# Taking the two-input passes of an attention layer off GpSimd: low weight parts by accumulating transfers, rotations and splits on VectorE

## The chip, the cores and the metric

The kernel runs on one core of a Trainium2 chip. A core has TensorE (matrix products; its weight loads are a second row, PEld, in the profile), VectorE (DVE), ScalarE (ACT), GpSimd (POOL) and SyncE (SP, which issues transfers). Each engine takes its own instructions strictly in the order of the program; engines wait for each other by semaphores. The metric is the time of the program on the device in microseconds (us), the median of several runs.

## The reference

Two layers over 512 positions of width 1024, in float32: a recurrent layer with a feed-forward block, then attention with a feed-forward block. What the change touches is the attention:

```python
k = rms_norm(k, k_norm[:, None, :]);  k = apply_partial_rope(k, cos, sin)      # shared_kv
q = (h @ w_q).reshape(B, S, N_GROUPS, Q_HEADS, HEAD_DIM)      # 3 groups, 8 heads of 128
q = rms_norm(q, q_norm[:, None, :])
q = apply_partial_rope(q, cos, sin)           # the first 32 of 128: x1*c - x2*s, x2*c + x1*s
...
for g, (window, dilation) in enumerate(DILATION_GROUPS):      # (128,1), (512,4), (2048,16)
    o, l = dilated_window_attention(q[:, :, g], k[:, :, g], v[:, :, g], window, dilation)
o = sum over g of softmax(l)[g] * o[g]
return o.reshape(B, S, Q_HEADS * HEAD_DIM) @ w_o
```

## The kernel before

Every product is made of three: each operand is split into a high part (a cast to TensorE's float32 format) and a low part (the rest), and high x high, high x low and low x high are summed. Weights come from DRAM in pieces of 128 x 1024 in one fixed order (`pieces`, a `Stream`): SP loads a piece into `wr` (two buffers, L78), ACT casts it to `wh` (L92), and the low part `wl` is made in one of three ways, by the piece's kind: on VectorE (`wr - wh`, L99), on GpSimd (the same line, kind "pool"), or, kind "dma", by ACT writing the negated cast (L95) and an accumulating transfer that GpSimd issues, which adds the weights from DRAM once more (L96). `wh` and `wl` have three buffers each. `get(i)` asks for the loads up to piece i + 2 and the splits up to piece i + 1. Kind "dma" is used before the change by eight pieces of the recurrent layer; the 24 pieces of `w_q` and the 8 of `w_o` are of kind "pool".

The attention goes so. First keys and values of three groups are projected. Then `project_q(0)` projects the queries of the first key/value head, three groups of four pieces (numbers 104 to 115): 24 products a piece, L641 to L643, from 604 to some 706 us. A group's four results are copied (`kn`, L579), ACT makes 16 sums of squares (`junk`, L583), VectorE the factors (L592, then L196 to L201) and the rotations: per result four scalings (L600) and four small two-input steps (L607 to L610). Each rotated result is transposed by TensorE (L716) and copied by ACT to `qt` (L718). The second head's projection, `project_q(1)` (pieces 116 to 127), is then mixed with the scores and values of the first head (L761 to L816: score tiles `pr`, minima `mn`, sums `den`, their transposes L786 and the split parts `ph`, `pl`), and the second head's scores with the two halves of the output projection (pieces 128 to 135, `out_half`). `query_parts` splits four heads' queries at a time into `qh` and `ql`, 24 times; before the change 16 of the low parts are made on GpSimd. For the second head the steps L607 to L610 (argument `E` of `normed`) are on GpSimd as well, 12 rotations.

The order on each engine is not written out by hand: the program is recorded and then put in order by a scheduler that goes by its own costs, with the splits of the weights at high priority. Names in the rows: `ps` a TensorE result bank, `qr4y` a factor, `grow` the gains, `ra` and `rbt` the small steps' tiles, `kh`/`kl` the keys' parts.

Of the kernel before, what the change touches and what calls it, by code (L numbers as in the profile page):

```python
# [127 lines left out]
def trunk(tc, A, out):  # L128
    nc = tc.nc
    V, S, G, PE = nc.vector, nc.scalar, nc.gpsimd, nc.tensor  # L130
# [9 lines left out]
    def add_pieces(aps, kind="", but=0):  # L140

        start = len(pieces)
        pieces.extend((a, "" if but and i % but == 0 else kind) for i, a in enumerate(aps))
        return start
# [6 lines left out]
    def ffn_pieces(wi, wo):  # L151
        a = add_pieces([A[wi][b] for j in range(HB) for b in (j, HB + j)])
        b = add_pieces([A[wo][m][:, c0:c1] for m in range(8) for c0, c1 in ((0, 1024), (1024, 2048), (2048, 2816))])
        return a, b

    p_f1 = ffn_pieces("f1_in", "f1_out")
    p_kv = add_pieces([A["w_kv"][i] for i in range(12)])
    p_q = add_pieces([A["w_q"][i] for i in range(24)], "pool")
    p_o = add_pieces([A["w_o"][i] for i in range(8)], "pool")
    p_f2 = ffn_pieces("f2_in", "f2_out")  # L160

    with tc.tile_pool(name="keep", bufs=1) as kp, tc.tile_pool(name="wts", bufs=3) as wp, \
# [7 lines left out]
        h = [kp.tile([128, T], F32, name=f"h{k}") for k in range(KB)]  # L170
# [88 lines left out]
        with tc.tile_pool(name="lru", bufs=2) as lp, \  # L259
# [149 lines left out]
            for i, m in enumerate(lru_order):  # L409
# [4 lines left out]
                while xs and xs[0][0] + 2 <= i:  # L414
                    st = xs.pop(0)[1]
# [69 lines left out]
def attention(tc, A, ap, ws, env):  # L485
    nc = tc.nc
    V, S, G, PE = nc.vector, nc.scalar, nc.gpsimd, nc.tensor
    h, xh, xl, ident, ssum = env["h"], env["xh"], env["xl"], env["ident"], env["ssum"]
    bank, mm3, split, halve, rsqrt = env["bank"], env["mm3"], env["split"], env["halve"], env["rsqrt"]
    gain, p_kv, p_q, p_o = env["gain"], env["p_kv"], env["p_q"], env["p_o"]  # L490
# [82 lines left out]
    def collect(raw, nh, t, st, copy):  # L573

        if t == 0:
            st["sq"] = ap.tile([128, 4 * nh], F32, name="sqc", tag=f"sqc{nh}").rearrange("q (t i) -> q t i", i=nh)
            st["kn"] = []
        dst = ap.tile([128, 512], F32, name="kn", tag="kn", bufs=N_KN)
        copy(dst[:, :128 * nh], raw[:, :128 * nh])  # L579
        junk = ap.tile([128, 128], F32, name="junk", tag="ra")  # L580
        for i in range(nh):
            c = slice(128 * i, 128 * i + 128)
            S.activation(junk, dst[:, c], AF.Square, accum_out=st["sq"][:, t, i:i + 1])  # L583
        st["kn"].append(dst)

    def normed(st, nh, tab, g_row, E, turn, lag):

        kn = st["kn"]

        def factors():  # L590
            sq = st["sq"]
            V.scalar_tensor_tensor(sq, sq, 1.0 / 128.0, epsv[:, tab:tab + 4].unsqueeze(2).to_broadcast([128, 4, nh]),  # L592
                                   ALU.mult, ALU.add)
            st["r"] = rsqrt(sq.rearrange("q t i -> q (t i)"), ap, f"qr{nh}")

        def rotate(t):
            dst, r = kn[t], st["r"]
            for i in range(nh):
                c = slice(128 * i, 128 * i + 128)
                V.scalar_tensor_tensor(dst[:, c], dst[:, c], r[:, nh * t + i:nh * t + i + 1], grow[:, g_row, :],  # L600
                                       ALU.mult, ALU.mult)
            x = dst.rearrange("q (h d) -> q h d", d=128)[:, :nh]
            a = ap.tile([128, 4, 32], F32, name="ra", tag="ra")[:, :nh]
            b = ap.tile([128, 4, 32], F32, name="rbt", tag="rbt", bufs=1)[:, :nh]
            cct = cc[:, tab + t].unsqueeze(1).unsqueeze(1).to_broadcast([128, nh, 2, 16])
            sst = [ss[:, tab + t, c, :].unsqueeze(1).to_broadcast([128, nh, 16]) for c in range(2)]
            E.tensor_tensor(*(v.rearrange("q h (c f) -> q h c f", c=2) for v in (a, x[:, :, 0:32])), cct, ALU.mult)  # L607
            E.tensor_tensor(b[:, :, 0:16], x[:, :, 16:32], sst[0], ALU.mult)
            E.tensor_tensor(b[:, :, 16:32], x[:, :, 0:16], sst[1], ALU.mult)
            E.tensor_tensor(x[:, :, 0:32], a, b, ALU.add)  # L610

        at(1, factors)
        for t in range(4):
            at(2 + t, lambda t=t: rotate(t))
            at(lag + t, lambda t=t: turn(t, kn[t]))
# [4 lines left out]
    def at(steps, fn):  # L620
        later.append((now[0] + steps, len(later), fn))
        later.sort(key=lambda e: e[:2])
# [6 lines left out]
    def project(p0, xh, xl, done):  # L629

        ps = [None] * 4
        for kk in range(4):
            wh, wl = ws.get(p0 + kk)
            for t in range(4):
                r = slice(128 * t, 128 * t + 128)
                if kk == 0:
                    ps[t] = bank()
                for k2 in range(2):
                    k = 2 * kk + k2
                    c = slice(512 * k2, 512 * k2 + 512)  # L640
                    PE.matmul(ps[t], xh[k][:, r], wh[:, c], start=k == 0, stop=False)  # L641
                    PE.matmul(ps[t], xh[k][:, r], wl[:, c], start=False, stop=False)  # L642
                    PE.matmul(ps[t], xl[k][:, r], wh[:, c], start=False, stop=k == 7)  # L643
                if kk == 3:
                    done(t, ps[t])
                tick()
                yield
# [58 lines left out]
    qt = {}  # L706

    def project_q(kv):
        for g in range(3):
            def done_q(t, ps, g=g, st={}):  # L710
                collect(ps, 4, t, st, V.tensor_copy)
                if t == 3:
                    def turn(j, rows):
                        pt = bank("PT")
                        for i in range(4):
                            PE.transpose(pt[:, 128 * i:128 * i + 128], rows[:, 128 * i:128 * i + 128], ident)  # L716
                        q = ap.tile([128, 4, 4, 32], F32, name="qt", bufs=12)
                        S.copy(q, pt.rearrange("q (h p i) -> q p h i", h=4, p=4))  # L718
                        qt[j, kv, g] = q

                    normed(st, 4, 0, 3 + g, G if kv else V, turn, 8 + kv)

            yield from project(p_q + 12 * kv + 4 * g, xh, xl, done_q)

# [4 lines left out]
    def query_parts(kv, n):  # L729
        qs_[kv, n] = []  # L730
        for g in range(3):
            if kv and n % 2:
                tags = (f"kh{g}0", f"kl{g}0", 1)
            else:
                tags = ("qh", "ql", 3)
            qh, ql = [ap.tile([128, 512], F32R, name=x, tag=x, bufs=tags[2]) for x in tags[:2]]
            halve(qt.pop((n, kv, g)).rearrange("q p h i -> q (p h i)"), qh, ql, V if g == kv else G)
            qs_[kv, n].append((qh, ql))

    def scores(kv, n, p):  # L740
        if p == 0 and (kv, n) not in qs_:
            query_parts(kv, n)
# [30 lines left out]
        if kv and p == 1 and n < 3:  # L773
            query_parts(kv, n + 1)
# [175 lines left out]
```

## Time and profile before

| | us |
|---|---|
| median of 3 runs (1265.87 to 1271.18) | 1268.6 |
| the profiled execution's own time | 1268.64 |
| its span, first to last instruction | 1266.9 |
| TensorE busy | 1218.9 (96%) |
| VectorE busy | 705.9 (56%) |
| ACT busy | 521.2 (41%) |
| GpSimd busy | 192.6 (15%) |

Busy times overlap; the span is set by the engine that is always needed. An average over the span hides stages: the attention lies between some 540 and 910 us. A timeline row is start, duration, engine, line, operation, output<-inputs, shape and count; in brackets stands how long the engine was idle before it and what ended that. `PEclk` is the granted share of TensorE's clock.

### The profile page before, as it was taken

The page shows a single profiled execution, that of the slowest core. Times are in us where ns is not written, and L with a number is a line of the kernel's source. Part 1 is how long each engine was busy: PE and PEld are TensorE (multiplying, and loading weights), DVE is VectorE, ACT ScalarE, POOL GpSimd, SP SyncE. Part 2 cuts the span into 40 slices and gives each one's busy share as a digit, 9 for nine tenths or more (in the row PEclk, how much of TensorE's full clock was granted, in tenths as well). Part 3 has the DMA queues.
Part 4 walks back from the last instruction along what each step waited for, and adds up shares of the span by engine and source line. Part 5 has one row for each costly group of instructions (what it writes and reads, how often), then busy time and mean ns, then how long its engine had stood idle before and what let it go on. Part 6 is the DMA issues. An engine that isn't in the chain of part 4 may idle for free.

```text
span 1266.9 us, 14906 instructions
## 1 busy us (share of the span) xinstructions
PE 1218.9 (96%) x5634; PEld 1010.3 (80%) x5634; DVE 705.9 (56%) x1292; ACT 521.2 (41%) x964; POOL 192.6 (15%) x172
## 2 busy tenths in 40 slices
PE   7899899999999999999998899899999999999998
PEld 6678688888888888887876777888888888888887
DVE  7788855554455333396566665785754455552221
ACT  5798532332322222266534554554432322332210
POOL 0100001111011000011333355422111011110000
PEclk9899999999999999999999999799999999999999
DMA  5454232223332333332422121001323332223431
GB/s 200 123 135 114 78 100 87 96 100 100 100 100 92 95 93 107 105 102 84 132 68 82 52 67 51 17 18 51 99 85 101 100 100 96 89 94 100 122 119 46
DMA packets 36649, 117.19 MB, mean 93 GB/s; under 512 B 4449, under 2 KB 6625, under 8 KB 36577
## 3 DMA queue, kind: packets, MB, share of 16 engines
q1 hardware_dynamic: 34416, 110.17, 27.6%
q0 software_dynamic: 1152, 4.19, 1.8%
q10 hardware_dynamic: 1008, 1.88, 0.5%
q8 instruction: 44, 0.72, 0.2%
q14 instruction: 29, 0.23, 0.1%
HBM read 113.08 MB, written 2.10 MB: 91 GB/s over the span
## 4 chain that ended last, share of the span: by engine, by line
PE 78%; DVE 12%; ACT 7%; issue 1%; DMA 1%; SPq 0%; DVEq 0%; ACTq 0%
PE ps L135 22%; PE ps L134 22%; PE ps L136 22%; DVE kn L600 3%; PE ps L641 3%; PE ps L643 3%; PE ps L642 3%; ACT junk L583 1%; ACT wh L92 1%; PE ps L716 1%; PE ps L786 1%; DVE kn L610 1%; DVE wl L99 1%; DVE pr L771 1%; DVE gated L386 1%
## 5 line engine op out<-in xcount | busy, mean ns | idle before, releaser
L92 ACT CAST wh<-wr 128x1024 fp32r<-128x1024 f32 (+2 forms) x206 | 210.9, 1024 | 506.8 <-PE ps L135 443.2
L134 PE MATMUL ps<-xh,wh 128*128 128x512 f32 x896 | 353.5, 395 | 12.1 <-ACT xh L205 6.0
L136 PE MATMUL ps<-xh,wl 128*128 128x512 f32 x896 | 351.1, 392 | 0.0
L135 PE MATMUL ps<-xl,wh 128*128 128x512 f32 x896 | 350.8, 391 | 0.0
L99 DVE TENSOR_TENSOR wl<-wr,wh 128x1024 fp32r<-128x1024 f32 (+2 forms) x166 | 240.0, 1447 | 151.9 <-ACT wh L92 151.8
L134 PEld LDWEIGHTS ps<-xh,wh 128*128 128x128 f32 x896 | 169.4, 189 | 48.2 <-DVE xp L332 6.3
L136 PEld LDWEIGHTS ps<-xh,wl 128*128 128x128 f32 x896 | 169.3, 189 | 35.6 <-issue 0.2
L135 PEld LDWEIGHTS ps<-xl,wh 128*128 128x128 f32 x896 | 169.5, 189 | 35.3 <-issue 0.5
L136 PE MATMUL ps<-gh,wl 128*128 128x512 f32 x352 | 137.1, 389 | 0.0
L134 PE MATMUL ps<-gh,wh 128*128 128x512 f32 x352 | 137.1, 389 | 0.0
L135 PE MATMUL ps<-gl,wh 128*128 128x512 f32 x352 | 137.1, 389 | 0.0
L451 POOL TENSOR_TENSOR u<-u,g 128x512 f32<-128x512 f32 x44 | 58.7, 1334 | 507.3 <-ACT wh L92 363.8
L450 DVE TENSOR_TENSOR u<-ps,rb 128x512 f32<-128x512 f32 x44 | 30.4, 691 | 139.2 <-PE ps L136 139.2
L99 POOL TENSOR_TENSOR wl<-wr,wh 128x1024 fp32r<-128x1024 f32 x32 | 77.1, 2409 | 193.2 <-ACT wh L92 141.8
L641 PE MATMUL ps<-wh,xh 128*128 128x512 f32 x224 | 93.2, 416 | 0.0
L643 PE MATMUL ps<-wh,xl 128*128 128x512 f32 x224 | 89.4, 399 | 0.0
L642 PE MATMUL ps<-wl,xh 128*128 128x512 f32 x224 | 89.1, 398 | 0.0
L134 PEld LDWEIGHTS ps<-gh,wh 128*128 128x128 f32 x352 | 66.1, 188 | 13.8
L136 PEld LDWEIGHTS ps<-gh,wl 128*128 128x128 f32 x352 | 66.1, 188 | 13.6
L135 PEld LDWEIGHTS ps<-gl,wh 128*128 128x128 f32 x352 | 66.1, 188 | 13.6
L448 DVE TENSOR_TENSOR g<-ps,rb 128x512 f32<-128x512 f32 x44 | 30.4, 691 | 63.9 <-PE ps L136 63.8
L209 ACT CAST gh<-u 128x512 fp32r<-128x512 f32 x44 | 27.4, 622 | 60.8 <-POOL u L451 60.8
(213 smaller groups left out, 1558.7 us busy)
## 6 DMA issues: line engine op xcount, KB each, us to landing
wr<-in_f_in SPq DMA_DIRECT2D x88, 512.0 KB, 3.5
wr<-in_f_out SPq DMA_DIRECT2D x32, 512.0 KB, 3.5
wr<-in_w_q SPq DMA_DIRECT2D x24, 512.0 KB, 3.5
wr<-in_w_in SPq DMA_DIRECT2D x14, 512.0 KB, 4.1
wr<-in_f_out SPq DMA_DIRECT2D x16, 384.0 KB, 3.1
wr<-in_w_kv SPq DMA_DIRECT2D x12, 512.0 KB, 3.5
wl<-in_w_in POOLq DMA_DIRECT2D x8, 512.0 KB, 7.2
wr<-in_a_out SPq DMA_DIRECT2D x8, 512.0 KB, 3.7
```

Of the source, the lines that this page charges most:

```text
L92: nc.scalar.copy(hi[:, c], r[:, c])
L99: eng.tensor_tensor(lo[:, c], r[:, c], hi[:, c].bitcast(F32), ALU.subtract)
L134: PE.matmul(ps, wh, xh, start=first, stop=False)
L135: PE.matmul(ps, wh, xl, start=False, stop=False)
L136: PE.matmul(ps, wl, xh, start=False, stop=last)
L448: V.tensor_tensor(g, pair[0], rb, ALU.mult)
L450: V.tensor_tensor(u, pair[1], rb, ALU.mult)
L451: G.tensor_tensor(u, u, g, ALU.mult)
L600: V.scalar_tensor_tensor(dst[:, c], dst[:, c], r[:, nh * t + i:nh * t + i + 1], grow[:, g_row, :], ALU.mult, ALU.mult)
L641: PE.matmul(ps[t], xh[k][:, r], wh[:, c], start=k == 0, stop=False)
L642: PE.matmul(ps[t], xh[k][:, r], wl[:, c], start=False, stop=False)
L643: PE.matmul(ps[t], xl[k][:, r], wh[:, c], start=False, stop=k == 7)
```

## The change

The pieces of `w_q` and `w_o` become kind "dma"; the rotations of both heads and all low parts of the queries go to VectorE.

```diff
-    p_q = add_pieces([A["w_q"][i] for i in range(24)], "pool")
-    p_o = add_pieces([A["w_o"][i] for i in range(8)], "pool")
+    p_q = add_pieces([A["w_q"][i] for i in range(24)], "dma")
+    p_o = add_pieces([A["w_o"][i] for i in range(8)], "dma")
...
-                    normed(st, 4, 0, 3 + g, G if kv else V, turn, 8 + kv)
+                    normed(st, 4, 0, 3 + g, V, turn, 8 + kv)
...
-            halve(qt.pop((n, kv, g)).rearrange("q p h i -> q (p h i)"), qh, ql, V if g == kv else G)
+            halve(qt.pop((n, kv, g)).rearrange("q p h i -> q (p h i)"), qh, ql)
```

The scheduler orders the new program afresh. TensorE's order stays the same up to the second head's projection. On ACT, in the second group of queries of the first head (pieces 113 to 115; `wr`, `wh`, `wl` the raw, high and low parts, `junk` the squares), this stood before:

```order
L92 CAST wh_5021<-wr_4946 128x1024
L583 ACTIVATE junk,sqc<-kn 128x128 x9
L92 CAST wh_5095<-wr_5019 128x1024
L583 ACTIVATE junk,sqc<-kn 128x128 x7
L92 CAST wh_5139<-wr_5093 128x1024
L718 COPY qt<-ps 128x512
```

and this now:

```order
L95 ACTIVATE wl_5031<-wr_4954 128x1024
L92 CAST wh_5030<-wr_4954 128x1024
L583 ACTIVATE junk,sqc<-kn 128x128 x9
L95 ACTIVATE wl_5106<-wr_5028 128x1024
L92 CAST wh_5105<-wr_5028 128x1024
L583 ACTIVATE junk,sqc<-kn 128x128 x7
L95 ACTIVATE wl_5151<-wr_5103 128x1024
L92 CAST wh_5150<-wr_5103 128x1024
L718 COPY qt<-ps 128x512
```

The multiplication stands ahead of the cast of its piece, once in the middle of the squares and once ahead of the copy of the transposed queries. For pieces 121, 122 and 128 to 135 the cast comes first.

On VectorE, in the second group of the second head's queries (around 762 us in the trace of before), with the score steps L761 and L764 that follow the rotations, before:

```order
L201 SCALAR_TENSOR_TENSOR qr4y<-qr4a,qr4y 128x16
L600 SCALAR_TENSOR_TENSOR kn<-kn,qr4y,grow 128x128 x12
L210 TENSOR_TENSOR pl<-ps,ph 128x3x128
L600 SCALAR_TENSOR_TENSOR kn<-kn,qr4y,grow 128x128 x4
L761 ISA pr,mn<-ps,near 128x256
L761 ISA mn 128x1
L764 ISA pr,mn<-ps,far,mn 128x256
```

and now, from the third rotation on (two whole rotations stand ahead of these rows):

```order
L607 TENSOR_TENSOR ra<-kn,cc 128x128
L608 TENSOR_TENSOR rbt<-kn,ss 128x4x16
L609 TENSOR_TENSOR rbt<-kn,ss 128x4x16
L600 SCALAR_TENSOR_TENSOR kn<-kn,qr4y,grow 128x128
L610 TENSOR_TENSOR kn<-ra,rbt 128x4x32
L600 SCALAR_TENSOR_TENSOR kn<-kn,qr4y,grow 128x128 x2
L761 ISA pr,mn<-ps,near 128x256
L761 ISA mn 128x1
L607 TENSOR_TENSOR ra<-kn,cc 128x128
L608 TENSOR_TENSOR rbt<-kn,ss 128x4x16
L609 TENSOR_TENSOR rbt<-kn,ss 128x4x16
L764 ISA pr,mn<-ps,far,mn 128x256
```

The small steps of the rotations now stand between the scalings, and the score steps behind three whole rotations.

## Rows read from the trace of the kernel before

**Rows 1.** Busy time by stretches: length, each engine's busy time, PEclk, DMA share, GB/s
```profile
600.00:706.00 106.00, 95.11 (x424) 77.17 (x423) 65.57 (x195) 47.51 (x159) 42.37 (x18) 0.95 0.29 90
706.00:850.00 144.00, 130.92 (x785) 115.40 (x785) 98.84 (x300) 80.78 (x236) 64.50 (x73) 0.93 0.13 41
```

**Rows 2.** Waits of TensorE, 600 to 850 us: total, times, longest
```profile
PE ps L716 <- DVE kn L610: 10.9, 6, 2.8
PE ps L786 <- DVE pr L771: 3.8, 3, 1.5
PE ps L135 <- DVE pl L210: 3.0, 1, 3.0
PE ps L134 <- DVE mn L764: 2.7, 1, 2.7
PE ps L716 <- POOL kn L610: 1.2, 1, 1.2
```

**Rows 3.** Stretches at half clock, columns as in rows 1
```profile
645.10:648.50 3.40, 3.40 (x10) 2.87 (x11) 0.00 (x0) 0.59 (x1) 0.00 (x0) 0.50 0.23 94
...
798.70:815.80 17.10, 14.72 (x68) 14.19 (x69) 16.04 (x47) 9.41 (x21) 9.39 (x18) 0.50 0.00 1
```

**Rows 4.** Timeline of VectorE in the second group of queries
```profile
661.63 3.54 DVE L600 SCALAR_TENSOR_TENSOR kn<-kn,qr4y,grow 128x128 f32<-128x128 f32 x5
...
666.03 0.87 DVE L600 SCALAR_TENSOR_TENSOR kn<-kn,qr4y,grow 128x128 f32<-128x128 f32 x3
666.81 0.29 DVE L607 TENSOR_TENSOR ra<-kn,cc 128x128 f32<-128x128 f32 x1
...
668.54 0.29 DVE L607 TENSOR_TENSOR ra<-kn,cc 128x128 f32<-128x128 f32 x1
...
669.01 1.39 DVE L600 SCALAR_TENSOR_TENSOR kn<-kn,qr4y,grow 128x128 f32<-128x128 f32 x1
670.32 2.42 DVE L610 TENSOR_TENSOR kn<-ra,rbt 128x128 f32<-128x128 f32 x1
```

**Rows 5.** Timeline of GpSimd: passes beside those steps
```profile
662.21 2.54 POOL L99 TENSOR_TENSOR wl<-wr,wh 128x1024 fp32r<-128x1024 f32 x1 [2.96 <-ACT wh L92]
...
670.21 2.38 POOL L99 TENSOR_TENSOR wl<-wr,wh 128x1024 fp32r<-128x1024 f32 x1
...
711.26 2.37 POOL L99 TENSOR_TENSOR wl<-wr,wh 128x1024 fp32r<-128x1024 f32 x1 [9.32 <-ACT wh L92]
```

**Rows 6.** Timeline of TensorE: a piece's first product, and two transposes that waited
```profile
632.19 0.39 PE L641 MATMUL ps<-wh,xh 128*128 128x512 f32 x1
...
666.25 0.63 PE L716 MATMUL ps<-ident,kn 128*128 128x128 f32 x4 [1.17 <-DVE kn L610]
...
672.88 1.09 PE L716 MATMUL ps<-ident,kn 128*128 128x128 f32 x4 [2.80 <-DVE kn L610]
```

**Rows 7.** Timeline of ACT: the cast of the piece that TensorE begins at 632.19
```profile
621.28 1.05 ACT L92 CAST wh<-wr 128x1024 fp32r<-128x1024 f32 x1 [0.55 <-PE ps L643]
```

**Rows 8.** The eight accumulating transfers of the recurrent layer (L96): ns, starts, landing
```profile
L96 POOL DMA_DIRECT2D wl<-in_w_in x8: 853/862/1011, 34.7 to 105.5; - x8
...
DMA to landing us min/median/max: 6.4/7.2/9.3
```

**Rows 9.** ACT's multiplications ahead of those transfers (L95): ns, starts
```profile
L95 ACT ACTIVATE wl<-wr x8: 1048/1052/1062, 33.3 to 104.2; 128x1024 fp32r<-128x1024 f32 x8
```

**Rows 10.** The queue of those eight transfers: packets, MB, share of 16 engines' span
```profile
q0 software_dynamic: 1152, 4.19, 1.8%
```

**Rows 11.** Timeline of VectorE: a half, a blocked step, scalings and factors of the second head
```profile
643.48 0.68 DVE L210 TENSOR_TENSOR ql<-qt,qh 128x512 fp32r<-128x512 f32 x1
...
711.63 2.15 DVE L771 TENSOR_SCALAR pr<-pr,den 128x256 f32<-128x256 f32 x1
...
762.49 4.20 DVE L600 SCALAR_TENSOR_TENSOR kn<-kn,qr4y,grow 128x128 f32<-128x128 f32 x12
...
795.31 0.41 DVE L592 SCALAR_TENSOR_TENSOR sqc<-sqc,epsv 128x16 f32<-128x16 f32 x1 [2.36 <-ACT junk L583]
```

## The prediction

> **What bounds the kernel now.** I read the busy time by stretches first, then what TensorE waited for in the attention layer, then the rows around those waits. TensorE is the bound: in the feed-forward layers it hardly pauses. The attention layer is where it loses time. From 600 to 706 us, the projection of the queries of the first key/value head, it is busy 95.1 of 106 us; from 706 to 850, where the second head's projection is mixed with the scores, 130.9 of 144 [rows 1]. All of the 10.9 us that the first stretch loses are six waits of the transposes at L716 for the last step of the rotation, DVE L610 [rows 2]. After such a wait the granted clock is 0.50 (1.2 of 2.4 GHz) for 3.4 us: the row at 645.1, two alike at 672.4 and 703.1, one at 771.4, and a long one of 17.1 us from 798.7 [rows 3].
>
> The rows say why the rotations are late. In the second group of queries five steps at L600 take 3.54 us from 661.63, where three take 0.87 at 666.03; one step at 669.01 takes 1.39 and the sum at 670.32 takes 2.42 [rows 4]. Each is stretched until a two-input pass on GpSimd ends: 662.21 to 664.75 and 670.21 to 672.59 [rows 5] (for the step at 669.01 it is a half of the queries, the pass before the second). TensorE then waits 1.17 us at 666.25 and 2.80 at 672.88 [rows 6].
>
> **What the change does, part by part.**
>
> *GpSimd's passes go.* The 32 low parts (2.4 us each, rows 5), 16 halves and 12 rotations leave GpSimd; it issues 32 transfers instead. What leaves it was not on the path by itself; the time it took from VectorE was. Five steps at L600 without a pass beside them take 0.87 + 2 x 0.27 = 1.4 us, so the second group loses 3.54 - 1.4 = 2.1, then 1.39 - 0.34 = 1.0, then 2.42 - 0.28 = 2.1: 5.2 us before its third rotation [rows 4]. TensorE's two waits there are 1.17 + 2.80 = 3.97 us [rows 6]; the third group has the same pattern, and 10.9 - 2 x 3.97 = 3.0 is left for the first [rows 2].
>
> *ACT gets 32 multiplications*, 1.05 us each [rows 9], ahead of the cast of the same piece. In each group one of them stands in the middle of the squares (the order above), so the factors and the rotations begin up to 1.05 us later. 5.2 - 1.05 = 4.1 us are given back in front of the third rotation where 3.97 was waited: it just fits. In front of the first rotation 2.1 - 1.05 = 1.05 stands against 1.17. So the six waits go, but for small remains, which I put at 1.0 us in all (bounds 0 and 4). With the waits the three slow stretches behind them go: TensorE was busy 3.4, 2.9 and 3.4 us at half clock, (3.4 + 2.9 + 3.4) x 0.5 = 4.8 us. First stretch: -10.9 - 4.8 + 1.0 = -14.7 us.
>
> *The transfers must land in time.* wl has three buffers. The multiplication for a piece starts when the piece three before is done, and the piece is used two pieces later: the cast of such a piece starts at 621.28 [rows 7] and its first product at 632.19 [rows 6], 10.9 us, so a piece takes 5.45 us. The new chain is 1.05 (multiplication) + 0.3 (handing over: the first and the last such issue start at 34.7 and 105.5, the multiplications before them at 33.3 and 104.2 [rows 8, 9]) + 7.2 us from issue to landing, the median of eight transfers of this kind and size that the recurrent layer makes now, 6.4 at least and 9.3 at most [rows 8]: 8.6 us, 10.7 at worst. Under 10.9 each time, so I cost it at nothing; the cover is 2.3 us in the middle and 0.2 at the worst. In the second stretch a piece has 15 us and more, since scores stand between. The last pieces of the output projection do the cast first, one 1.05 us more: 9.6, still under.
>
> Here a page speaks against the change. The Trainium skill, SBUF — State Buffer, section "SBUF: two separate sides", says that while VectorE runs an operation in a two-port mode GpSimd cannot write the descriptors of its transfers, and tells one to issue from another queue. By that rule an issue would wait for one VectorE operation, which in this stretch is under 0.7 us, and the chain would be 9.3 us and not 8.6: no wait either way. The Trainium skill, DMA: Bandwidth & Descriptors, section "Anatomy of one DMA — SWDGE (gpsimd) path", gives 2.0 us + bytes / 436e3, which for 512 KB is an estimate of 3.2 us. The eight landings at 6.4 to 9.3 say more than twice that for an accumulating transfer, and they decide.
>
> *SP.* The load of piece 108 moves ahead of eight small transfers at L685. It waits for ACT's cast of piece 106 where it waited for GpSimd, which ends earlier; behind it queue those eight, needed far later. Nothing, or a small gain. Loads in general are released by ACT's two operations (2.1 us) where it was a cast and a pass (1.05 + 2.4).
>
> *VectorE in the second stretch* gets 16 halves of 0.68 us [rows 11], 10.9 us, and 12 rotations. A rotation takes 1.73 us in all (666.81 to 668.54 [rows 4]); four steps at L600 are 0.87 + 0.27 = 1.14 of it, so 0.6 each is new, 7.2 us. Added: 18.1 us on 98.8 of 144 [rows 1]: 117, if none of the stretched time came back, so VectorE does not become the bound as a whole. Locally it can. Waits that go: the 3.8 us for L771, one of which is the pass of 2.15 us at 711.63 [rows 11] beside GpSimd's at 711.26 [rows 5], and 1.2 for GpSimd's own rotation; of these 5.0 us [rows 2] I take 4.0 (bounds 1.5 and 5.0). Wait that stays: 2.7 us for L764 [rows 2]. Before, 12 + 4 steps at L600 and a half stood in front of it, 4.20 us of them in one row [rows 11], some 6.2 us in all; now three whole rotations and the next one's steps, 3 x 1.73 + 1.14 = 6.3: no change. Wait that grows: 3.0 us for pl at L210 [rows 2]. It stands behind L592, which at 795.31 has waited 2.36 us for ACT's squares [rows 11], and two multiplications now lie among those squares: +1.0 (bounds 0 and 2.1). For the added halves and rotations between the score steps I take +2.5 (0 if all of it finds VectorE idle, 6 if a third of the 18 lands on the path). Second stretch: -4.0 + 1.0 + 2.5 = -0.5 us. The 17 us at half clock I leave as they are, since the 3.0 us wait in front of them stays.
>
> *Keys.* The casts of the transposed keys stand behind one more multiplication at two places; TensorE may wait once for its transpose bank: +0.5 (0 to 1.5).
>
> **Sum**, against the profiled execution's own time, 1268.6 us (its span and 1.7 around it; the median of the runs is the same): 1268.6 - 14.7 - 0.5 + 0.5 = 1253.9, so 1254 us, 1.2% less.
>
> **The rivals.**
>
> *A: the transfers land late, slower than before.* With three buffers the piece time cannot be under (1.35 + landing) / 2: 4.3 us at 7.2, 5.3 at 9.3, both under 5.45. From 9.6 us on TensorE waits at every piece. Some 15 pieces follow each other at full pace (12 of the first projection, the last three of the output). At 13 us the piece takes 7.2: 15 x 1.75 = 26 us lost, 1254 + 26 = 1280. It outweighs the gain of 14.7 from a landing of 11.5 us on (15 x 0.98), and is slower by over 0.5% from some 12.4. For it: such a transfer takes 1.8% of 1266.9 us over eight, 2.85 us of all 16 engines [rows 10], and loads take 0.29 of the time already [rows 1], 1.6 us a piece: 4.4 of 5.45 us. Against it: two of the eight were issued within 3 us of each other and still landed in 9.3. Chance 0.07.
>
> *B: ACT holds the gain back.* The multiplication delays the squares by 1.05, and then the copies of the transposed queries too, which stand behind the next multiplication and cast, and the transposes wait for these. If half of the six waits is left, and with it the slow clock behind the larger ones, the first stretch gives 7 us: 1262. For it: my balance above fits by 0.1 us only. Against: the copies have a margin of over 1 us. Chance 0.15.
>
> *C: VectorE becomes the bound between 780 and 850.* Eight of the halves and a group of rotations fall there. If the added work costs 10 and not 2.5, 1262. Chance 0.11.
>
> *D: the second stretch gains too.* All 5.0 us go and the long slow clock is halved: 1254 - 1 - 3.5 - 4.3, about 1245. Chance 0.10.
>
> **How the numbers follow.** The forecast has 0.57, from 1248 to 1259. A measurement tells about 0.5% from no change, 6.3 us: faster is under 1262.3, slower above 1274.9. B and C lie on that line, so half of each is faster: 0.57 + 0.10 + 0.13 = 0.80. Same: the other half and the milder part of A, 0.15. Slower 0.05. The range goes from 1242 (D and the remains at zero) to 1266 (B or C and the upper bounds of the second stretch), and leaves A and the tail of both out.
>
> **What would show it.** Right: no wait of L716 for L610 above 1 us before 706, L600 at 0.34 us throughout, a clock of 1.00 from 640 to 706, the piece at 5.45 us, landings of 7 to 8 us. Wrong: waits of the products at L642 for a landing (A), of L716 for ACT's copy at L718 (B), of L786 or L135 for DVE above 3 us after 780 (C).

## The result, and the profile after

The changed kernel takes **1252.7 us** (median of four executions, 1252.0 to 1258.0), the kernel before 1267.8: a ratio of 0.989, 95% interval [0.985, 0.992]. The forecast was 1254, faster. The profiled execution is the longest of the four, 1258.0 us; a second profile of the same kernel, taken with the experiments below, took 1254.1, and both are read here.

Busy time, and the queue of the accumulating transfers, on the page of the first profile [rows 10]:

```profile
PE 1222.4 (97%) x5634; PEld 1014.8 (81%) x5634; DVE 680.5 (54%) x1356; ACT 550.1 (44%) x996; POOL 101.9 (8%) x108
...
q0 software_dynamic: 5760, 20.97, 10.0%
```

VectorE has more instructions and less busy time than before (705.9 us). The work that moved to it is smaller than the time that it no longer spends standing still.

Busy time by stretches in the first profile, columns as in [rows 1], whose two stretches stand first; then the three stretches at half clock, which answer to [rows 3]:

```profile
600.00:706.00 106.00, 103.87 (x500) 85.70 (x500) 54.59 (x220) 72.89 (x212) 14.68 (x17) 1.00 0.83 183
706.00:850.00 144.00, 136.96 (x796) 123.33 (x795) 98.19 (x365) 86.51 (x225) 9.52 (x11) 0.87 0.36 80
...
754.80:758.20 3.40, 3.40 (x19) 3.40 (x18) 1.86 (x7) 2.82 (x5) 0.86 (x1) 0.50 0.13 31
782.10:788.90 6.80, 6.80 (x35) 6.80 (x34) 6.73 (x33) 3.63 (x8) 0.00 (x0) 0.50 0.06 12
792.30:819.60 27.30, 26.39 (x119) 25.17 (x118) 17.69 (x58) 11.08 (x29) 0.00 (x0) 0.50 0.00 1
```

The first stretch is now full: TensorE is busy 103.9 of 106 us at the full clock. VectorE is busy 11 us less there. In the second stretch half clock lasts 37.5 us, where it was 20.5. The second profile shows 27.3 us in three parts, and one more part in the first stretch, behind a wait of 1.87 us at 638:

```profile
639.80:643.20 3.40, 3.40 (x11) 2.75 (x10) 3.40 (x16) 2.98 (x4) 0.86 (x1) 0.50 0.46 133
...
755.80:759.20 3.40, 3.40 (x15) 3.21 (x15) 1.23 (x6) 2.70 (x5) 0.86 (x1) 0.50 0.32 89
783.10:796.80 13.70, 12.19 (x57) 11.34 (x57) 13.52 (x56) 9.06 (x18) 0.00 (x0) 0.50 0.00 1
803.60:813.80 10.20, 10.20 (x48) 9.91 (x48) 6.41 (x26) 4.75 (x15) 0.00 (x0) 0.50 0.00 0
```

TensorE's waits from 600 to 850 us in the second profile, columns as in [rows 2]:

```profile
PE ps L135 <- DVE pl L210: 3.1, 2, 1.6
PE ps L716 <- DVE kn L610: 1.9, 1, 1.9
PE ps L134 <- ACT ph L209: 1.8, 2, 1.2
PE ps L134 <- DVE mn L764: 1.6, 1, 1.6
PE ps L786 <- DVE pr L771: 0.8, 1, 0.8
PE ps L716 <- DVE pl L210: 0.8, 1, 0.8
```

Of the six waits of L716 for L610, 10.9 us, one is left. The second group of queries shows why, on VectorE (first profile) and on TensorE, where the four transposes now wait for nothing [rows 4, 6]:

```profile
660.91 1.40 DVE L600 SCALAR_TENSOR_TENSOR kn<-kn,qr4y,grow 128x128 f32<-128x128 f32 x5
...
666.16 0.34 DVE L600 SCALAR_TENSOR_TENSOR kn<-kn,qr4y,grow 128x128 f32<-128x128 f32 x1
666.42 0.28 DVE L610 TENSOR_TENSOR kn<-ra,rbt 128x128 f32<-128x128 f32 x1
```

```profile
665.24 0.60 PE L716 MATMUL ps<-ident,kn 128*128 128x128 f32 x4
667.06 0.60 PE L716 MATMUL ps<-ident,kn 128*128 128x128 f32 x4
```

The five steps at L600 take 1.40 us where they took 3.54, the single one 0.34 (1.39), the sum at L610 0.28 (2.42).

Stage times, in us, between the first products of the named pieces in the traces. Pieces 104 to 115 are the first head's queries, 116 to 127 the second's. The second column ends with the last product of line L641, the third begins with it:

| kernel | 104 to 120 | 120 to last L641 of the queries | from there to last L786 | end of span |
|---|---|---|---|---|
| before | 115.5 | 70.9 | 81.6 | 1266.9 |
| changed, first profile | 99.7 | 68.3 | 87.9 | 1256.3 |
| changed, second profile | 101.0 | 68.1 | 83.7 | 1252.3 |
| weights only | 100.9 | 74.2 | 81.4 | 1257.0 |
| weights and rotations | 100.7 | 73.1 | 82.2 | 1254.7 |
| weights and halves | 99.4 | 69.9 | 83.4 | 1253.4 |
| moves only | 109.1 | 72.5 | 82.2 | 1264.4 |
| weights on VectorE | 100.7 | 68.3 | 84.8 | 1253.1 |

Behind these stages the traces agree within 0.7 us; from the first product of its norm on, the last feed-forward block takes 359.4 to 359.9 us in all of these kernels. Ahead of them piece 104 begins anywhere from 603.4 to 605.7 us, and of this spread 1.8 us arise before the first product of the keys and values, in a part that none of the edits touches. So the stages are compared and not the spans.

### The profile page after: what moved, and what is told of

Its sections match the earlier page's. It is cut to its first block, busy times and chain, and to the rows that moved or that the text cites. A ratio compares the mean times of both kernels' runs of the same rounds, so it can differ in the third digit from the quotient of the medians.

```text
span 1256.3 us, 14918 instructions
## 1 busy us (share of the span) xinstructions
PE 1222.4 (97%) x5634; PEld 1014.8 (81%) x5634; DVE 680.5 (54%) x1356; ACT 550.1 (44%) x996; POOL 101.9 (8%) x108
## 4 chain that ended last, share of the span: by engine, by line
PE 79%; ACT 8%; DVE 8%; DMA 3%; issue 1%; SPq 0%; DVEq 0%; ACTq 0%
PE ps L135 23%; PE ps L136 23%; PE ps L134 23%; PE ps L641 3%; PE ps L642 3%; PE ps L643 3%; ACT junk L583 2%; DMA wr<-in_w_q 2%; ACT wh L92 1%; DVE kn L600 1%; ACT wl L95 1%; PE ps L716 1%; DVE wl L99 1%; PE ps L786 1%; DVE gated L386 1%
## 5 line engine op out<-in xcount | busy, mean ns | idle before, releaser
L136 PE MATMUL ps<-xh,wl 128*128 128x512 f32 x896 | 351.1, 392 | 0.0
L136 PEld LDWEIGHTS ps<-xh,wl 128*128 128x128 f32 x896 | 169.5, 189 | 35.7 <-issue 0.2
L136 PE MATMUL ps<-gh,wl 128*128 128x512 f32 x352 | 136.9, 389 | 0.0
L641 PE MATMUL ps<-wh,xh 128*128 128x512 f32 x224 | 91.2, 407 | 0.0
L642 PE MATMUL ps<-wl,xh 128*128 128x512 f32 x224 | 87.4, 390 | 0.0
L136 PEld LDWEIGHTS ps<-gh,wl 128*128 128x128 f32 x352 | 66.1, 188 | 13.8
L134 PEld LDWEIGHTS ps<-gh,wh 128*128 128x128 f32 x352 | 66.1, 188 | 13.7
L135 PEld LDWEIGHTS ps<-gl,wh 128*128 128x128 f32 x352 | 66.1, 188 | 13.6
L209 ACT CAST gh<-u 128x512 fp32r<-128x512 f32 x44 | 27.3, 621 | 62.0 <-POOL u L451 62.0
L95 ACT ACTIVATE wl<-wr 128x1024 fp32r<-128x1024 f32 x40 | 42.2, 1056 | 19.0 <-PE ps L642 12.3
```

Source lines behind the costliest of these rows:

```text
L95: nc.scalar.mul(lo[:, c], r[:, c], -1.0)
L134: PE.matmul(ps, wh, xh, start=first, stop=False)
L135: PE.matmul(ps, wh, xl, start=False, stop=False)
L136: PE.matmul(ps, wl, xh, start=False, stop=last)
```

## The experiments

The theory: what cost the time was GpSimd's passes stretching VectorE's steps, not the passes' own lateness. The rivals: the gain belongs to the moved rotations and halves; or to the transfers themselves; or ACT's multiplications hold part of it back; or the landings are close to being late.

### The changed kernel again

> The changed kernel once more, for a second profile. Its first profile gained 15.8 us between 604 and 705 us and lost 6.3 us in the last stretch of the attention, where 27 us ran at half clock; its other executions were 5 us quicker than that profile. Expected: 1252 to 1254 us; the first stretch as in the first profile (its pieces 104 to 120 in some 100 us, no half clock, no wait of the transposes L716 for L610 above 1 us); the last stretch, from the last product of the queries to the last transpose L786, at 82 to 85 us and not 87.9. If it is 88 again, the loss belongs to the change and not to that execution.

Measured: 1254.5 us, ratio 0.991 [0.989, 0.993]. The last stage took 83.7 and not 87.9. So the first profile's long stretch at half clock varies between executions of one program, and some 4 us of it belong to that execution; 2 us more than before the change remain. One expectation was missed: the wait of L716 that ends at 638 to 640 us is there in both profiles (2.13 us in the first, 1.87 in the second), and in the second 3.4 us at half clock follow it.

### Weights only, moves only

The first is the kernel before with the upper two lines, the second the changed kernel with the lower two:

```diff
+    p_q = add_pieces([A["w_q"][i] for i in range(24)], "dma")
+    p_o = add_pieces([A["w_o"][i] for i in range(8)], "dma")
...
+    p_q = add_pieces([A["w_q"][i] for i in range(24)], "pool")
+    p_o = add_pieces([A["w_o"][i] for i in range(8)], "pool")
```

> Only the 32 weight pieces go over to accumulating transfers; rotations of the second head and 16 halves of the queries stay on GpSimd. Theory (the gain comes from GpSimd's two-input weight passes no longer stretching VectorE's steps): the first stretch (pieces 104 to 120) gains 13 to 16 us as in the full change, since only two half passes of 2 us remain there; the second stretch stays as before or is 1 to 4 us worse than the full change; 1253 to 1259 us. Rival (the moved rotations and halves carry the gain): 1262 to 1268 us.

> Only the rotations and halves go to VectorE; the 32 weight passes stay on GpSimd. Theory: the first stretch keeps its waits of L716 for L610 (8 to 11 us) and its slow clock, and the second stretch puts 18 us more of work on a VectorE that is still stretched by passes: 1264 to 1274 us. Rival (the moves carry the gain): 1252 to 1258 us.

Measured: weights only 1259.2 us, 0.994 [0.992, 0.995]; moves only 1265.3, 0.998 [0.997, 0.999]. With the weights alone the first stage gains all of its 14.6 us, and the second stage loses 3.3. With the moves alone the waits for L610 are there still, 9.1 us in six:

```profile
PE ps L716 <- DVE kn L610: 9.1, 6, 1.9
PE ps L786 <- DVE pr L771: 9.1, 4, 5.5
```

and VectorE's steps at L600 are as long as in [rows 4]:

```profile
661.78 3.55 DVE L600 SCALAR_TENSOR_TENSOR kn<-kn,qr4y,grow 128x128 f32<-128x128 f32 x5
```

Summed over 600 to 706 us, VectorE's steps take 18.3 us more before the change than the same steps take in the changed kernel. With the moves alone the excess is 16.1 us, with the weights alone 2.3. So the theory stands for these waits: the weight passes made them.

One expectation was missed. The slow clock of the first stage did not stay with the moves alone:

```profile
600.00:706.00 106.00, 96.90 (x461) 78.98 (x459) 65.50 (x202) 51.79 (x165) 39.35 (x16) 1.00 0.28 90
```

The granted clock is 1.00 over the whole stretch, though three of the waits are 1.84 to 1.93 us long; before the change 10.2 us ran at half clock there. So the moves alone shorten the first stage as well, by 6.4 us: 1.8 us less waiting, and some 5 by the clock (half of the 10.2 us). Why the clock held was not settled. The two edits alone give 8.8 and 2.7 us, 11.5 in sum, and together 13.6 to 15.1: the moves seem to be worth more once the passes are gone, but the difference is no larger than the spread within some of the programs.

### Weights on VectorE: neither pass nor transfer

```diff
+    p_q = add_pieces([A["w_q"][i] for i in range(24)])
+    p_o = add_pieces([A["w_o"][i] for i in range(8)])
```

> No pass on GpSimd and no transfer either: the 32 low parts are made on VectorE (about 1 us each where nothing disturbs it, 4 us of the 22 us of a group), rotations and halves there too. Theory (what counts is that GpSimd makes no two-input pass; the transfer is only one way): first stretch as in the changed kernel within 2 us; VectorE's 32 us of added work costs 0 to 6 us in the second stretch; 1251 to 1260 us. Rival (the gain hangs on the transfer, through an earlier release of the raw piece or VectorE's time): 1262 us or more. Rival B of the prediction (ACT's multiplications hold some gain back): this kernel has none, and would be quicker than the changed kernel by 1 to 4 us.

Measured: 1253.1 us, 0.989 [0.988, 0.991], the same as the changed kernel. The transfers are one way to free GpSimd and carry no gain of their own: VectorE itself has room for the 32 low parts. Without ACT's multiplications the waits for L610 from 600 to 706 us are 1.4 us in four, none over 0.5, and the kernel is no quicker. So rival B's gain did not show, but this run cannot rule it out: VectorE's 32 added passes may have cost what the missing multiplications gave.

### Every transfer twice

```diff
-                    nc.scalar.mul(lo[:, c], r[:, c], -1.0)
+                    nc.scalar.mul(lo[:, c], r[:, c], -2.0 if i >= 104 else -1.0)
-                    nc.gpsimd.dma_start(lo[:, c], self.pieces[i][0][:, c], accum_op=ALU.add)
+                    nc.gpsimd.dma_start(lo[:, c], self.pieces[i][0][:, c], accum_op=ALU.add); i >= 104 and nc.gpsimd.dma_start(lo[:, c], self.pieces[i][0][:, c], accum_op=ALU.add)
```

> The changed kernel with every accumulating transfer of the 32 attention pieces made twice, the second behind the landing of the first (ACT writes minus twice the cast, so the low parts come out doubled and the output is a little off); the order on all engines is otherwise the same. It doubles the cost that rival A of the prediction rests on. Rival A's formula, piece time = (1.35 + landing) / 2: the chain becomes 1.35 + 2 x 7 = 15.4 us and with a second handing over some 16, so a piece takes about 8 us where it took 5.45; over some 15 pieces 35 to 40 us are lost: 1285 to 1300 us, and more if the clock falls behind each wait (up to 1330). TensorE's new waits stand at the products of L642 and at the second products L135 of the output projection, for a transfer. If landing times are hidden in some other way that the formula does not see: 1253 to 1260 us.

Measured, one execution: 1309.6 us. TensorE's waits, and the landings:

```profile
PE ps L642 <- DMA wl<-in_w_q: 36.1, 18, 4.4
```

```profile
DMA to landing us min/median/max: 5.2/7.3/10.1
```

The loss is 55 us: 43 in the first stage (144.0 us for 16 pieces where the changed kernel takes 101.0), 11 in the last pieces of the output projection, which follow each other without anything between; there TensorE waits 7.1 us at L136. In the first 16 pieces GpSimd issues a piece's first transfer every 8.1 to 10.8 us, 8.9 in the mean, where the formula of rival A gives 8. GpSimd's timeline shows what sets this period:

```profile
630.67 1.76 POOL L96 DMA_DIRECT2D wl<-in_w_q  x2 [6.71 <-DMA wl<-in_w_q]
638.76 1.76 POOL L96 DMA_DIRECT2D wl<-in_w_q  x2 [6.33 <-DMA wl<-in_w_q]
```

A row holds the second transfer of one piece and the first of the next. GpSimd, which takes its instructions in order, stands still until a piece's first transfer has landed. For pieces 105 to 128 the first issue comes 0.82 or 0.83 us after the landing of the first transfer of the piece before, 24 times out of 24. So the period is a landing and 0.8 us, set by GpSimd's queue, and not by the three buffers of rival A's formula, which this run therefore does not test. What it shows is where TensorE waits when low parts come late, at L642, and that this is costly. The time lies above the expected 1285 to 1300 us and inside the 1330 that were allowed for the clock: 44 us ran at half clock from 600 to 860 us, where the second profile above has 31.

### The negation on GpSimd

```diff
-                    nc.scalar.mul(lo[:, c], r[:, c], -1.0)
+                    (nc.gpsimd.tensor_scalar(lo[:, c], r[:, c], -1.0, None, ALU.mult) if i >= 104 else nc.scalar.mul(lo[:, c], r[:, c], -1.0))
```

> The changed kernel with the negated cast of the 32 attention pieces on GpSimd in place of ACT: a pass with one input in front of each transfer, on the engine that issues it (GpSimd's one-input casts of 128x512 took 0.62 us in the changed kernel, so about 1.2 us each). Theory (only GpSimd's two-input passes stretch VectorE): VectorE's steps keep their length, ACT has 33 us less, the squares come about 1 us earlier in each group, and the one wait of the transposes near 638 us (2.1 us) shrinks: 1249 to 1254 us. Rival (any pass of GpSimd over such a tile stretches VectorE): VectorE's excess in 600 to 706 us comes back to half of before or more (8 us and up) and the waits of L716 for L610 with it: 1257 to 1265 us.

Measured: 1256.9 us, 0.991 [0.990, 0.993]. Both guesses were off. The pass took 2.77 us and not 1.2, more than a pass with two inputs (2.4, [rows 5]):

```profile
640.46 2.77 POOL L95 TENSOR_SCALAR wl<-wr 128x1024 fp32r<-128x1024 f32 x1 [1.48 <-PE ps L642]
```

It does stretch VectorE, but in this stretch no pass holds more than one step, and only by 0.8 to 0.9 us (eight of the 17 passes that start between 600 and 706 us do so):

```profile
640.52 1.00 DVE L199 TENSOR_TENSOR qr4a<-qr4y,sqc 128x16 f32<-128x16 f32 x1
641.56 0.18 DVE L200 SCALAR_TENSOR_TENSOR qr4a<-qr4a,qr4y 128x16 f32<-128x16 f32 x1
```

The step that starts with the pass takes 1.00 us for 0.18, the next ones run at their own speed while the pass goes on to 643.2. From 600 to 706 us VectorE's steps take 7.2 us more than the same steps in the changed kernel (18.3 before). The kernel's order also came out different on TensorE, with waits of 5.4 us for L771 and 4.1 for the keys' kl, so that its time cannot be put down to the passes alone.

### Which of the two moves counts

Each is the changed kernel with one line: halves back on GpSimd, then rotations back on GpSimd:

```diff
+            halve(qt.pop((n, kv, g)).rearrange("q p h i -> q (p h i)"), qh, ql, V if g == kv else G)
...
+                    normed(st, 4, 0, 3 + g, G if kv else V, turn, 8 + kv)
```

> The changed kernel with 16 of the halves of the queries back on GpSimd; weights by transfers and rotations on VectorE stay. With the weights alone the kernel took 1259.2 us, with all three edits 1252.7 to 1254.5; this run and the next split the 4.7 us (or more) between halves and rotations. Theory (the rotations matter more, since their 48 small passes on GpSimd lie on the way to the transposes): 1253 to 1256 us, with one or two steps of VectorE stretched by a half pass in the first stretch. Rival (the halves matter more: 2 us each beside VectorE): 1256 to 1260 us.

> The changed kernel with the 12 rotations of the second head back on GpSimd; weights by transfers and halves on VectorE stay. Theory (rotations matter more): 1256 to 1260 us, the stretch from piece 116 to the last product of the queries at 100 us and more, where the changed kernel has 95.4. Rival (the halves matter more): 1253 to 1256 us. If neither of the two runs is near the changed kernel, the two moves work only together.

Measured: with the halves on GpSimd 1259.8 us, 0.993 [0.992, 0.995], as if the weights alone had gone over; with the rotations on GpSimd 1253.6, 0.988 [0.986, 0.990], the changed kernel's time. My theory was the wrong way round: the halves' move is worth some 6 us, the rotations' nothing. GpSimd and VectorE with the halves on GpSimd, at the second head's factors:

```profile
709.45 2.53 POOL L210 TENSOR_TENSOR ql<-qt,qh 128x512 fp32r<-128x512 f32 x2 [1.53 <-ACT qh L209]
```

```profile
709.49 1.28 DVE L196 TENSOR_SCALAR qr4y<-sqc 128x16 int32<-128x16 int32 x1
...
710.95 1.07 DVE L197 TENSOR_SCALAR qr4y<-qr4y 128x16 int32<-128x16 int32 x1
712.06 0.18 DVE L199 TENSOR_TENSOR qr4a<-qr4y,sqc 128x16 f32<-128x16 f32 x1
```

Two passes, one behind the other, hold two steps of 0.17 us for 1.28 and 1.07. The twelve factor steps follow each other strictly and the rotations stand behind them. TensorE's waits that end at 721 us (L716 for pl) and 757 (for L764) are 1.9 and 3.8 us in this trace, 0.8 and 1.6 in the second profile of the changed kernel, which fits; that each lost microsecond is passed on was not shown step by step. A rotation on GpSimd stretches VectorE's scalings too (5.3 us from 706 to 800), but it takes 0.6 us of work off VectorE at the same place. Over 706 to 850 us VectorE's steps are stretched by 10.5 us with the halves on GpSimd and by 5.9 with the rotations there. The scheduler made a new order for each of the two programs, so the 6 us are those of edit and order together.

The Trainium skill, SBUF — State Buffer, section "SBUF: two separate sides", has VectorE and GpSimd share one pair of ports as an exclusive lock for a whole instruction. The second of the steps above ends at 710.95 + 1.07 = 712.02 us and the two passes at 709.45 + 2.53 = 711.98, which agrees; under the negation the step ended 1.7 us before the pass did, which does not.

### Score steps first

In `scores` the steps from the minima L761 to the division L771, with ACT's exponential, and in `turned` the split into ph and pl go under the scheduler's high priority:

```diff
+        with tc.high_priority():
+            V.tensor_tensor_reduce(pr[:, :g0], ps[:, :g0], near[:, p, 256 - g0:256], 1.0, 3e38,
...
-        halve(pt.rearrange("q (b k) -> q b k", k=128)[:, :nb], ph[:, :nb, p % 2], pl[:, :nb, p % 2])
+        with tc.high_priority(): halve(pt.rearrange("q (b k) -> q b k", k=128)[:, :nb], ph[:, :nb, p % 2], pl[:, :nb, p % 2])
```

> The changed kernel with the score steps of VectorE and ACT (minima, exponential, division) and the parts ph, pl of the probabilities put ahead of rotations and halves that are ready at the same time. In the second profile of the changed kernel the waits of 1.2 to 1.6 us at 754, 780 to 782, 792 and 803 us are all for such steps, and 27 us at half clock follow them. Theory (the order on VectorE and ACT makes these waits): the waits for mn L764 and pl L210 fall from 4.7 us to under 2, half clock to under 14 us, 1244 to 1250 us. Rival (the rotations that now come later hold the transposes L716 up instead): 1253 to 1260 us.

> The kernel before with the score steps and the parts of the probabilities put first, as in the run that gained 6 us on the changed kernel. Theory (that gain is one of order and has nothing to do with GpSimd): 1260 to 1264 us. Rival (the order helps only where GpSimd's passes no longer stretch the steps that were put first): 1266 to 1271 us. In both the waits of L716 for L610 from 600 to 706 us stay at some 11 us.

Measured on the changed kernel: 1248.1 us, 0.983 [0.980, 0.985]; on the kernel before: 1275.4, 1.006 [1.005, 1.007]. Waits in the first of the two (two lines are numbered one higher there):

```profile
PE ps L716 <- DVE kn L610: 4.5, 4, 1.8
PE ps L135 <- DVE pl L210: 1.6, 1, 1.6
PE ps L134 <- ACT ph L209: 1.2, 1, 1.2
PE ps L787 <- DVE pr L772: 1.2, 1, 1.2
```

The wait for mn L764 is gone and the one for pl halved; the transposes L716 wait 2.6 us more in return. The larger effect is on the clock: 13.7 us at half clock instead of 27.3, which at half speed is 6.8 us. These are single profiles, and in the changed kernel two profiles differed by 10 us at half clock in this stretch. On the kernel before the same edit makes things worse, by more than either theory gave. The waits for L610 stay at 10.9 us in six, as both expected, and half clock rises from 31 to 41 us. So the gain is not one of order alone; why the order costs so much beside GpSimd's passes was not settled. In that trace the wait for mn (L765 there) is 4.3 us where it was 2.7, and one of 1.9 us for VectorE's ql is new. Nor was it tried which of the two priorities does the work.

### The output projection on VectorE, alone and with the score steps first

```diff
+    p_o = add_pieces([A["w_o"][i] for i in range(8)])
```

> The changed kernel with the eight pieces of the output projection split on VectorE; the 24 of the queries stay with transfers. At 775 us one multiplication and one cast for the first of these pieces stand in the middle of the squares of the last group on ACT, and TensorE waits 1.2 us for ACT's ph at 780. Theory (the eight transfers are not where the gain comes from, and ACT's multiplications there cost up to 1 us): 1251 to 1254 us, the same within the measurement. Rival (the transfers of the output projection carry part of the gain): 1256 us or more.

> The changed kernel with score steps and parts first, and the eight pieces of the output projection split on VectorE in place of ACT's multiplication and a transfer. Score steps first alone: 1248.1 us; these pieces on VectorE alone: 1252.9, no measurable difference. Theory (with the waits for VectorE shortened, ACT's two operations for the first of these pieces, in the middle of the squares at 775 us, are what is left): 1244 to 1247 us. Rival (VectorE's eight passes of 1 us fall between the score steps instead): 1248 to 1252 us.

Measured: alone 1252.9 us, 0.988 [0.986, 0.990], no difference from the changed kernel; together with the score steps first **1244.2**, 0.982 [0.980, 0.984] (1242.6 to 1252.1 in five executions). The wait for ACT's ph is 0.2 us in the profile, where it was 1.8 in the second profile of the changed kernel and 1.2 with the score steps first alone; the one for pl grew from 1.6 to 2.8:

```profile
PE ps L716 <- DVE kn L610: 4.2, 3, 2.2
PE ps L135 <- DVE pl L210: 2.8, 1, 2.8
...
PE ps L134 <- ACT ph L209: 0.2, 1, 0.2
```

Its interval lies below the changed kernel's, and the one of score steps first overlaps it: that version is quicker than both kernels, and whether the output projection adds to it stays open. The profiled execution is the longest of the five, with 27 us at half clock; the spread of 10 us within one program is larger than this last step.

## Why the prediction was right, point by point

**The total.** Forecast 1254 us, measured 1252.7. That it came within 1.3 us is partly luck: the profiled execution took 1258.0 and the median of a second set 1254.5, and below terms of both signs are off by 1 to 9 us. The mechanism and the size of the first stretch, which carry the gain, were right.

**The first stretch.** Forecast -14.7 us, measured -15.8 and -14.5 (pieces 104 to 120). These two hold 1.5 us that the forecast put down to the second stretch, a wait for L771 that ended at 713.9 us before the change; without it they are -14.3 and -13.0. The balance held where it was made: in the second and third groups nothing waits any more. The remains were put at 1.0 us (0 to 4). They are one wait of 1.9 to 2.1 us in the first group, once with 3.4 us at half clock behind it, so 2.1 to 3.6 us.

**SP: a step that failed.** I costed the new place of the load of piece 108 at "nothing, or a small gain". SP's queue in the second profile (SPq: when it issues its transfers), and before, where the last row begins with the loads of 108 and 109:

```profile
609.78 0.54 SPq L78 DMA_DIRECT2D wr<-in_w_q  x1
610.42 3.02 SPq L685 DMA_DIRECT2D vh<-ph  x4
613.53 3.65 SPq L685 DMA_DIRECT2D vl<-pl  x4
617.28 18.38 SPq L78 DMA_DIRECT2D wr<-in_w_q  x5
```

```profile
613.10 30.40 SPq L78 DMA_DIRECT2D wr<-in_w_q  x7
```

The load of 108 went ahead of eight small transfers, and that of 109 now stands behind them, at 617.3 us where it was at 613.7, right behind 108's at 613.1. ACT, in its strict order, waited for it with the squares behind; then VectorE's factors waited for the squares, and TensorE for the rotation (second profile, timelines of ACT, VectorE and TensorE):

```profile
623.64 1.06 ACT L95 ACTIVATE wl<-wr 128x1024 fp32r<-128x1024 f32 x1 [2.83 <-DMA wr<-in_w_q]
```

```profile
633.46 0.17 DVE L592 SCALAR_TENSOR_TENSOR sqc<-sqc,epsv 128x16 f32<-128x16 f32 x1 [4.92 <-ACT junk L583]
```

```profile
638.37 0.66 PE L716 MATMUL ps<-ident,kn 128*128 128x128 f32 x4 [1.87 <-DVE kn L610]
```

I had looked at who needs the eight transfers, and not at what stands behind them. The place in the queue is not all of it. The loads of the weights themselves land later beside the new transfers. From issue to landing, loads of `w_q` issued from 590 to 706 us, before and in the second profile:

```profile
DMA to landing us min/median/max: 3.4/3.5/5.1
```

```profile
DMA to landing us min/median/max: 3.4/6.5/8.5
```

The sum had no term for this; with the weights on VectorE and no transfer the median is 3.4 us. The load of 109 landed 4.4 us after its issue before and 6.3 in the second profile, at 623.5 and not at 618.1. Of these 5.40 us, 3.55 are the place in the queue and 1.85 the slower landing.

The kernel with the weights on VectorE has SP's order of before, no transfer and no multiplication, and no such wait, so it does not separate the load from the multiplications. Eight traces do, those of the changed kernel and of the experiments that keep ACT's multiplications and single transfers:

| trace | ACT idle before L95 of piece 109, us | wait of L716 that follows, us |
|---|---|---|
| output projection on VectorE | 2.44 | 1.51 |
| weights and rotations | 2.48 | 1.53 |
| weights only | 2.71 | 1.75 |
| score steps first | 2.74 | 1.80 |
| changed, second profile | 2.83 | 1.87 |
| weights and halves | 2.89 | 1.93 |
| changed, first profile | 3.10 | 2.13 |
| score steps first, output projection on VectorE | 3.17 | 2.21 |

TensorE's wait is ACT's idle time less 0.93 to 0.97 us each time, so it follows the lateness of the load. By this line, which is an estimate outside of 2.44 to 3.17 us, an idle time under 0.95 us would have left no wait with the multiplications in place, and either of the load's two delays alone would have left next to none.

**The transfers.** All 40 transfers of the first profile, against 6.4/7.2/9.3 in [rows 8], and ACT's multiplications, against [rows 9]:

```profile
L96 POOL DMA_DIRECT2D wl<-in_w_q x24: 858/865/878, 594.7 to 746.6; - x24
...
L96 POOL DMA_DIRECT2D wl<-in_w_o x8: 865/865/865, 756.7 to 876.9; - x8
...
who waited for it (us, times):
...
DMA to landing us min/median/max: 6.0/7.0/9.6
```

```profile
L95 ACT ACTIVATE wl<-wr x40: 1044/1057/1064, 34.1 to 875.6; 128x1024 fp32r<-128x1024 f32 x40
```

Nobody waited for a landing; the share of the transfer engines, put at 4.4 of 5.45 us or 0.81, is 0.83. The cover was as thin as forecast: by the trace, the transfers of pieces 105 and 109 landed 0.5 and 0.3 us ahead of their first use. Rival A did not come about. Doubling the transfers shows that low parts which come late are costly (55 us there), but not by rival A's formula: the period was set by GpSimd's queue. What the transfers did cost is the slower landing of the loads above.

**The second stretch.** Forecast -0.5 us; -0.7 in the second profile (151.8 after 152.5 us from piece 120 to the last L786), +3.7 in the first; with the 1.5 us of the wait at 713.9, which belong here, -2.2 and +2.2. That -0.7 came so near is luck: several terms were off, with both signs. The waits that were to go went (3.8 us for L771 to 0.8, 1.2 for GpSimd's rotation to none: -4.2, forecast -4.0). The one for L764 fell from 2.7 to 1.6 where I had it unchanged, the one for pl stayed at 3.1, now in two, where I had 4.0; one of 1.0 us for L770, which I had not named, went. For the added work between the score steps I had 2.5 us. The waits for ACT's ph and of L716 for pl are 2.6 us in sum, but 1.1 of them were there before, so 1.5 came. The long slow clock was the mis-sized term: I left it at 17 us, 20.5 with the one at 771, and it came to 27 and 37 us, 3 to 9 us of time. In the second profile it follows waits of 1.2 to 1.6 us, at 754, 780 to 782 and 803, and not the one wait of 3.0 that I had tied it to.

**Keys.** Forecast +0.5 us; the projection of keys and values took 0.5 longer in the first profile and 0.5 less in the second.

**Which edit does what.** The sum had one term for halves and rotations together. The runs give the halves some 6 us and the rotations none; the trace shows a half's pass of 1.3 us holding a step of 0.2 us to its end, which fits, though the new order of each program is part of the difference.

**Rivals B and C.** The second and third groups, where ACT's multiplications stand among the squares too, wait for nothing. VectorE did not become the bound as a whole, yet the order of its steps is worth 5 to 6 us there, as the runs with the score steps first show; that is the part of C which was right.

## What to carry to other kernels

Before an idle engine is given a long pass, see in the trace what the short steps on the neighbouring engine do during it: here steps of 0.2 to 0.3 us took up to 2.4. Of a transfer that moves in a queue, ask also what now stands behind its new neighbours; of new transfers, what they do to the landing of the old ones (here 3.5 us became 6.5). Where short waits bring long stretches at half clock, count the stretch and not the wait: waits of 1.2 to 1.6 us were followed by 3.4 to 13.7 us at half speed.

## What was not expected of the hardware

- A multiplication by a constant on GpSimd (128x1024, one input) took 2.77 us, more than its pass with two inputs (2.4 us) and ACT's 1.05. Where a VectorE step met it from 600 to 706 us, it stretched that one step by 0.8 to 0.9 us and no other, where a pass with two inputs held steps to its end.
- A step with one input is stretched like one with two: L196 on 128x16 integers took 1.28 us beside a pass of the halves, 0.17 without.
- The clock does not follow from one wait alone: after 2.13 us at 637 it stayed at 1.00 in the first profile of the changed kernel, after 1.87 us at 636 it fell to 0.50 for 3.4 us in the second. With the moves alone it stayed at 1.00 after three waits of 1.84 to 1.93 us, where before the change it fell after one of 1.90.
- Beside the accumulating transfers plain loads of 512 KB took 6.5 us from issue to landing, 3.5 without them (medians).
- Of two accumulating transfers to the same tile the second landed in 5.2 to 5.7 us in 12 of the first 16 pieces, where the first took 7.2 to 10.0.
